# The first tile's result leaves by channels and comes back in squares of 32 tokens

## The chip, the core and the metric

The kernel runs on one core of a Trainium2 chip, as one program launched once. Five engines work side by side, each through a list of instructions of its own in a fixed order: TensorE (PE in the profile, its weight loads PEld), VectorE (DVE), ScalarE (ACT), GpSimd (POOL) and SyncE (SP). They wait for each other on semaphores. DMAs are issued from an engine's list, nearly all of them here from SyncE's. On-chip memory (SBUF, and PSUM for what TensorE writes) has 128 partitions. The metric is the device time of one execution in microseconds.

## What is computed

The reference is one step of a small streaming encoder of two layers, for a prompt of 1024 frames and a sample of 32 frames that share their weights. Rows are frames (tokens), columns are 1024 channels. Cut to what matters here:

```
def trunk(x, c, pool_cache, ...):
    for i in range(DEPTH):                       # 2 layers
        sh1, sc1, gt1, sh2, sc2, gt2 = split(silu(c) @ w_ada[i] + b_ada[i])
        h = rmsnorm(x, g_norm[i, 0]) * (1 + sc1) + sh1
        mix = sgu_mixer(h, ...) if i % 2 == 0 else pool_mixer(h, ...)
        x = x + gt1 * rmsnorm(mix, g_norm[i, 1])
        h = rmsnorm(x, g_norm[i, 2]) * (1 + sc2) + sh2
        f = square(relu(h @ ffn_w_up[i])) @ ffn_w_down[i]      # 1024 -> 4096 -> 1024
        x = x + gt2 * rmsnorm(f, g_norm[i, 3])
    return x
```

The last line of the loop, in the second layer, gives the outputs y_prompt (1024 x 1024) and y_sample (32 x 1024), rows of tokens. All values are 32-bit floats.

## The kernel before, in words

**Layout.** On chip the activations stand by channels: partition p of block k holds channel 128k + p, and the tokens lie along the free dimension. The tokens are cut into three tiles (TILES, L27): tile 0 and tile 1 of 384 prompt tokens, tile 2 of 256 prompt tokens and the 32 sample tokens. `acc[t]` holds the running sums of tile t, 8 blocks of 128 channels. The outputs are rows of tokens, so a result has to be turned once before it is written.

**The FFN, which is most of the time.** Each of its products runs as three matmuls of rounded parts (high times high, high times low, low times high), so that float precision is kept. The inner width of 4096 is cut into eight chunks of 512. One item (`ffn_item`, L1333) is one chunk for one tile: four `up` steps (pf, matmuls L917 to L919, then ScalarE's relu and square and a split into fh and fl), and a `down` of eight output blocks (pg), which VectorE adds into `acc`. The `down` of an item is issued after the first `up` of the next, so TensorE does not wait for the split. In layer 1 the last chunks, 6 and 7, go first for tiles 0 and 1, then for tile 2 (L344, L345). So the items at the end are: chunk 7 of tile 0, chunk 7 of tile 1, chunk 6 of tile 2, chunk 7 of tile 2.

**Weights.** They arrive in 512 KB pieces through three slots named raw (`t_raw`, L165, RAW_SLOTS) on SyncE's queue (L427); ScalarE makes the high part (L440), VectorE the low part. The same three raw slots also hold finished rows (yo) before they are written.

**The end of a tile.** After a tile's last `down`, `to_out` (L1614) puts a generator into `fillers`; its steps are recorded between the FFN's steps by `weave` and `pull`, which count TensorE's and VectorE's work in `time` and hold a step that yields a number back by so many counted microseconds. For tiles 0 and 1 the generator runs `residual` (L819): the norm's factor, the scaling of `acc`, and the addition of the old activations, which SyncE loads from DRAM in four pieces (xo_r, L826). Then, per block of 128 tokens, TensorE turns 8 squares of 128 x 128 into PSUM (yT, L1677), ScalarE copies them to a raw slot (yo, L1678), and SyncE writes 512 KB (L1679). That is 24 transpositions, six copies and three writes per tile.

**Tile 2** is last and goes another way (`last`, L1623). Its old activations were written by channels to DRAM scratch (xtd, L1437), are loaded back in squares of 32 tokens by 32 channels (`load_last`, L1395, nine loads) into the room that tile 0's inputs left, and VectorE turns each 32 x 32 square in place of TensorE (`turn_x`, L1405, VectorE's 32-wide transposition). The tile's sums are turned by TensorE while the last `down` runs (`turn_last`, L1420, yT at L1426). Once the norm's factor is known (r_last), one operation per half block scales and adds (xlast), and the rows are written (L1655, L1661).

**Buffers and order.** A buffer is named by a tag with a number of slots; a new buffer waits until the slot's last user is done. PSUM for transpositions has three slots (`ps_ms`, L142). Outside the hand-ordered opening, the framework's planner puts the recorded instructions in an order on each engine when the kernel is built, by costs and finishing times of its own; on the chip that order does not change. A DMA takes one of eight completion semaphores in turn, so it also waits for the DMA eight before it.

Of the kernel before, what the change touches and what calls it, by code (L numbers as in the profile page):

```python
# [9 lines left out]
F32 = mybir.dt.float32  # L10
# [5 lines left out]
P = 128  # L16
D = 1024
KB = D // P
# [5 lines left out]
HALO = 16  # L24
# [10 lines left out]
def tile_stream_encoder_step(  # L35
# [25 lines left out]
    nc = tc.nc  # L61
# [11 lines left out]
    def on_dve(op, fixed, rate):  # L73
        def run(out, *args, **kw):
            n = 1
            for k in out.shape[1:]:
                n *= k
            time["dve"] += fixed + n / rate
            return op(out, *args, **kw)  # L79

        return run
# [4 lines left out]
    turn32 = on_dve(nc.vector.transpose, 0.1, 930.0)  # L86
# [7 lines left out]
    dram = pool("dram", space=bass.MemoryType.DRAM)  # L94


    ncol = [p + s for _, p, s in TILES]
# [5 lines left out]
    acc = [const.tile([P, KB, HALO + n], F32, name=f"acc{t}") for t, n in enumerate(ncol)]  # L103
    xd = [dram.tile([P, KB, n], F32, name=f"xd{t}") for t, n in enumerate(ncol)]
    vd = dram.tile([SEQ + DEC, SGU], F32, name="vd")


    LAST = [(0, 0, P), (P, 0, P), (ncol[-1] - P, P - DEC, DEC)]
    xtd = dram.tile([32, 4, KB, ncol[-1]], F32, name="xtd")

    ident = const.tile([P, P], F32, name="ident")
    make_identity(nc, ident)
# [8 lines left out]
    part = const.tile([P, 4, NV, 8], F32, name="part")  # L121
# [11 lines left out]
    def room(part, t, name, dtype=F32):  # L133
        return work.tile([P, KB, ncol[t]], dtype, tag=f"h{part}{t}", bufs=1, name=name)
# [30 lines left out]
    def t_raw(name):  # L165
        return work.tile([P, 1024], F32, tag="raw", bufs=RAW_SLOTS, name=name)
# [652 lines left out]
    def residual(st, l, cf, tag, out, store=True, stat=True):  # L819
        t = st.t  # L820
        n = ncol[t]
        xos = {}

        def load(k2):
            xos[k2] = t_x(f"xo_{tag}_{k2}", [P, 2, n])
            nc.sync.dma_start(xos[k2], xd[t][:, 2 * k2 : 2 * k2 + 2, :])  # L826

        got = []
        yield from st.finish(got)
        r = got[0]  # L830
        st2 = Stat(t, tag + "x")
        for half in range(2):
            for k2 in (2 * half, 2 * half + 1):
                load(k2)
            for k2 in (2 * half, 2 * half + 1):
                for k in (2 * k2, 2 * k2 + 1):
                    for c0, w, v in segs[t]:
                        a = A(t, k, c0, w)
                        stt(
                            out=a,  # L840
                            in0=a,
                            scalar=coef[:, l, cf, v, k : k + 1],
                            in1=r[:, c0 : c0 + w],
                            op0=ALU.mult,
                            op1=ALU.mult,
                        )
                    yield True
                a = acc[t][:, 2 * k2 : 2 * k2 + 2, HALO:]
                tt(out=a, in0=a, in1=xos[k2], op=ALU.add)
                if stat:  # L850
                    st2.square(2 * k2, a)
                yield k2 % 2 == 0
        if store:
            nc.sync.dma_start(xd[t], acc[t][:, :, HALO:])
        out.append(st2)
# [246 lines left out]
    for half in range(2):  # L1102
        x = work.tile([P, 384], F32R, tag="rr", bufs=2, name=f"hs{half}")[:, : 8 * DEC].rearrange(
            "p (k n) -> p k n", k=4
        )
# [227 lines left out]
    def ffn_item(p, t, after):  # L1333
# [17 lines left out]
        def down():  # L1351
            for d in range(KB):
# [11 lines left out]
                if after is not None:  # L1364
                    st.square(d)
                    if l == 1 and t == NT - 1:
                        scale_last(d)
                        if d < len(LAST):
                            turn_x(d)
# [18 lines left out]

    last_ps = {}

    def rows_last(part, name):
        x = room(part, 0, name).rearrange("p k n -> p (k n)")
        return x.rearrange("p (b d) -> p b d", d=D)

    def load_last():  # L1395

        last_ps["raw"] = rows_last("l", "xraw")
        for i, (c0, r0, nr) in enumerate(LAST):
            for r in range(r0, r0 + nr, 32):
                nc.sync.dma_start(  # L1400
                    last_ps["raw"][r : r + 32, i].rearrange("p (j m) -> p j m", m=32),
                    xtd[:, :, :, c0 + r : c0 + r + 32].rearrange("s a k m -> s (a k) m"),
                )

    def turn_x(i):  # L1405
        if i == 0:
            last_ps["x"] = rows_last("h", "xlast")
        _, r0, nr = LAST[i]
        turn32(
            last_ps["x"][r0 : r0 + nr, i].rearrange("p (k a s) -> p a k s", k=KB, a=4),  # L1410
            last_ps["raw"][r0 : r0 + nr, i].rearrange("p (a k m) -> p a k m", a=4, k=KB),
        )

    def scale_last(d):
        t = NT - 1
# [4 lines left out]
    def turn_last(d):  # L1420
        half = d // 4
        for i, (c0, _, _) in enumerate(LAST):
            if d % 4 == 0:
# [6 lines left out]
    def mix_to_ffn(st, l):  # L1430
        t = st.t
        out = []
        need_ada(l, 2)
        yield from residual(st, l, 1, f"r1_{l}_{t}", out, store=l == 0 or t < NT - 1)
        if l == 1 and t == NT - 1:
            for a in range(4):
                nc.sync.dma_start(xtd[:, a], acc[t][32 * a : 32 * a + 32, :, HALO:])  # L1437
        need_ada(l, 4)
        yield from modulate(out[0], l, 2, 3)

# [173 lines left out]
    def to_out(st):  # L1614
        t = st.t
        col0, npr, nsm = TILES[t]
        blocks = [
            (c * P, P, y_prompt[0, col0 + c * P : col0 + (c + 1) * P, :]) for c in range(npr // P)
        ]
        if nsm:  # L1620
            blocks.append((npr, nsm, y_sample[0]))

        def last():  # L1623

            turn_last(KB - 2)
            pn = ps_dn("pn_last")
            nb = len(LAST)
            for k in (0, KB - 1):
                if k > 0:
                    turn_last(KB - 1)  # L1630
                for i, (c0, _, _) in enumerate(LAST):
                    mm(
                        pn[:, 2 * i : 2 * i + 2],
                        st.sq[:, k, c0 : c0 + P],
                        ones[:, 0:2],
                        start=k == 0 and i == 0,
                        stop=k > 0 and i == nb - 1,
                        skip_group_check=True,
                    )
            sums = pn[:, : 2 * nb].rearrange("p (b c) -> p b c", c=2)[:, :, 0]  # L1640
            r, q = (t_st(f"{x}_last")[:, :nb] for x in ("r", "q"))
            act(out=r, in_=sums, func=AF.Abs_reciprocal_sqrt, scale=1.0 / D)
            tt(out=q, in0=r, in1=r, op=ALU.mult)
            stt(out=q, in0=sums, scalar=-0.5 / D, in1=q, op0=ALU.mult, op1=ALU.mult)
            stt(out=r, in0=q, scalar=1.5, in1=r, op0=ALU.add, op1=ALU.mult)
            xt = last_ps["x"]
            dsts = [dst for _, _, dst in blocks]
            for i, (_, r0, nr) in enumerate(LAST):
                rows = slice(r0, r0 + nr)
                for half in range(2):  # L1650
                    d = slice(half * 512, half * 512 + 512)
                    y, x = last_ps[(i, half)][rows, :], xt[rows, i, d]
                    if nr == P:
                        stt(out=x, in0=y, scalar=r[rows, i : i + 1], in1=x, op0=ALU.mult, op1=ALU.add)
                        nc.sync.dma_start(dsts[i][:, d], x)  # L1655
                        continue

                    z = t_x(f"zlast{half}", [P, 512])[rows, :]
                    act(out=z, in_=y, func=AF.Copy, scale=r[rows, i : i + 1])
                    nc.gpsimd.tensor_tensor(out=x, in0=z, in1=x, op=ALU.add)  # L1660
                    nc.scalar.dma_start(dsts[i][:, d], x)  # L1661
            yield False

        def run():
            need_ada(1, 5)
            if t == NT - 1:
                yield from last()
                return
            yield from residual(st, 1, 3, f"r2_1_{t}", [], store=False, stat=False)
            yield 0.5  # L1670
            for c0, w, dst in blocks:
                tick(1.0)
                yo = t_raw(f"yo{t}_{c0}")
                for half in range(2):
                    pt = ps_ms(f"yT{t}_{c0}_{half}")
                    for i in range(4):
                        nc.tensor.transpose(pt[:w, i * P : (i + 1) * P], A(t, half * 4 + i, c0, w), ident)  # L1677
                    act(out=yo[:w, half * 512 : (half + 1) * 512], in_=pt[:w, :], func=AF.Copy)  # L1678
                nc.sync.dma_start(dst, yo[:w, :])  # L1679
                yield False  # L1680

        fillers.append((f"out_{t}", run()))

    run_ffn(1, to_out)
# [46 lines left out]
```

## Time and profile before

| | us |
|---|---|
| median of three runs | 2165.44 (2163.97 to 2165.93) |
| the profiled execution | 2163.59 |
| its span, first to last instruction | 2161.8 |
| TensorE busy in the span | 2143.9 (99%) |
| VectorE busy | 1423.9 (66%) |
| ScalarE busy | 981.9 (45%) |
| GpSimd busy | 7.9 |
| DMA | 311.77 MB, 144 GB/s on average |

In the profile's rows an operation is named by its source line, its engine, and out<-in by the program's buffer names; xN is a count. L79 is the line of a helper through which VectorE's operations pass, so names tell them apart. A row of the timeline begins with its start in the span and its length, and ends with the idle time ahead of it and what ended that. "SPq" is the issue of a DMA on SyncE's queue; landing is the time from issue until the DMA has signalled completion. Matmul lengths are modelled and overlap; the distance between the starts of two rows is the better measure of what a matmul costs.

### The profile page before, as it was taken

How to read it: one execution, taken by the hardware profiler on the slowest of the kernel's cores; microseconds unless marked ns; L12 is line 12 of the kernel's file. 1: busy time of each engine (PE TensorE's matmuls, PEld its weight loads, DVE VectorE, ACT ScalarE, POOL GpSimd, SP SyncE). 2: the span in 40 equal slices, each digit the busy share in tenths (PEclk: the TensorE clock that was granted, in tenths of full speed). 3: DMA queues.
4: the chain of work that ended last, by engine and by line, in shares of the span. 5: the costliest groups of instructions: out<-in, count | busy, mean ns of one | idle time of the engine just before them, and what ended most of it. 6: DMA issues, size and time to landing. Idle time of an engine off the chain costs nothing.

```text
span 2161.8 us, 33186 instructions
## 1 busy us (share of the span) xinstructions
PE 2143.9 (99%) x13214; PEld 2079.8 (96%) x13214; DVE 1423.9 (66%) x2520; ACT 981.9 (45%) x1667; POOL 7.9 (0%) x20
## 2 busy tenths in 40 slices
PE   8999999999999999999999999999999999999998
PEld 6878999999999999999999999999999999999998
DVE  6787738467778549576757779869685553523375
ACT  5634332233456652324345566656564542322454
POOL 0000000000000000000000000000000000000000
PEclk9999999999999999999999999999999999999999
DMA  8486524353447444344545466465454541302243
GB/s 299 153 269 209 168 82 136 96 153 107 133 126 220 127 147 146 98 117 137 175 127 164 143 192 200 148 193 164 141 161 133 166 149 58 108 20 69 78 137 120
DMA packets 363263, 311.77 MB, mean 144 GB/s; under 512 B 20099, under 2 KB 325803, under 8 KB 363109
## 3 DMA queue, kind: packets, MB, share of 16 engines
q1 hardware_dynamic: 362852, 309.43, 46.6%
q8 instruction: 103, 1.69, 0.3%
q14 instruction: 52, 0.42, 0.1%
q10 hardware_dynamic: 128, 0.14, 0.0%
q0 software_dynamic: 128, 0.09, 0.0%
HBM read 278.95 MB, written 30.66 MB: 143 GB/s over the span
## 4 chain that ended last, share of the span: by engine, by line
PE 96%; DVE 2%; DMA 1%; ACT 1%; issue 0%; POOL 0%; POOLq 0%; ACTq 0%; DVEq 0%
PE pf L917 11%; PE pg L917 11%; PE pf L919 11%; PE pf L918 11%; PE pg L919 11%; PE pg L918 11%; PE pu L917 3%; PE pu L919 3%; PE pu L918 3%; PE po L917 3%; PE po L918 3%; PE po L919 3%; PE pv L943 2%; PE pv L944 2%; PE pv L945 2%; PE psp L1263 1%
## 5 line engine op out<-in xcount | busy, mean ns | idle before, releaser
L917 PE MATMUL pg<-fh,wh_dn 128*128 128x384 f32 (+1 forms) x1536 | 496.1, 323 | 0.0
L917 PE MATMUL pf<-hh,wh_up 128*128 128x384 f32 (+1 forms) x1536 | 494.4, 322 | 0.0
L919 PE MATMUL pf<-hh,wl_up 128*128 128x384 f32 (+1 forms) x1536 | 493.0, 321 | 1.2 <-DVE wl_up L79 1.2
L918 PE MATMUL pf<-hl,wh_up 128*128 128x384 f32 (+1 forms) x1536 | 493.1, 321 | 0.0
L918 PE MATMUL pg<-fl,wh_dn 128*128 128x384 f32 (+1 forms) x1536 | 492.5, 321 | 0.0
L919 PE MATMUL pg<-fh,wl_dn 128*128 128x384 f32 (+1 forms) x1536 | 492.5, 321 | 0.0
L79 DVE TENSOR_TENSOR wl_up<-raw,wh_up 128x1024 fp32r<-128x1024 f32 x152 | 185.8, 1223 | 169.1 <-ACT wh_up L440 169.1
L919 PEld LDWEIGHTS pf<-hh,wl_up 128*128 128x128 f32 x1536 | 288.6, 188 | 1.9 <-DVE wl_up L79 1.9
L917 PEld LDWEIGHTS pg<-fh,wh_dn 128*128 128x128 f32 x1536 | 288.3, 188 | 1.5 <-ACT fh L1169 0.4
L440 ACT ACTIVATE wh_up<-raw 128x1024 fp32r<-128x1024 f32 x152 | 161.2, 1060 | 282.3 <-PE pf L918 217.7
L918 PEld LDWEIGHTS pg<-fl,wh_dn 128*128 128x128 f32 x1536 | 288.3, 188 | 0.9 <-DVE fl L79 0.2
L918 PEld LDWEIGHTS pf<-hl,wh_up 128*128 128x128 f32 x1536 | 288.3, 188 | 0.4
L917 PEld LDWEIGHTS pf<-hh,wh_up 128*128 128x128 f32 x1536 | 288.2, 188 | 0.4
L919 PEld LDWEIGHTS pg<-fh,wl_dn 128*128 128x128 f32 x1536 | 288.2, 188 | 0.0
L79 DVE TENSOR_TENSOR acc<-acc,pg 128x384 f32<-128x384 f32 (+1 forms) x336 | 173.7, 517 | 151.2 <-PE pg L919 150.5
L440 ACT ACTIVATE wh_dn<-raw 128x1024 fp32r<-128x1024 f32 x152 | 160.9, 1060 | 209.8 <-PE pg L918 171.4
L79 DVE TENSOR_TENSOR wl_dn<-raw,wh_dn 128x1024 fp32r<-128x1024 f32 x152 | 185.8, 1223 | 82.7 <-ACT wh_dn L440 82.6
L79 DVE SCALAR_TENSOR_TENSOR aa<-raw,csil,aa 128x512 f32<-128x512 f32 (+1 forms) x364 | 203.2, 619 | 7.6 <-DMA raw<-in_w_ada_dram 7.3
L1345 ACT ACTIVATE r<-pf 128x384 f32<-128x384 f32 (+1 forms) x192 | 86.5, 450 | 197.7 <-PE pf L919 197.7
L79 DVE TENSOR_TENSOR fl<-r,fh 128x384 fp32r<-128x384 f32 (+1 forms) x192 | 100.0, 521 | 85.7 <-ACT fh L1169 84.2
L917 PE MATMUL pu<-hh,wh_u 128*128 128x384 f32 (+1 forms) x384 | 125.9, 328 | 0.0
L917 PE MATMUL po<-ush,wh_o 128*128 128x384 f32 (+1 forms) x384 | 123.5, 322 | 0.0
(268 smaller groups left out, 2923.2 us busy)
## 6 DMA issues: line engine op xcount, KB each, us to landing
raw<-in_ffn_w_up_dram SPq DMA_DIRECT2D x152, 512.0 KB, 3.9
raw<-in_ffn_w_down_dram SPq DMA_DIRECT2D x152, 512.0 KB, 3.5
raw<-in_w_ada_dram SPq DMA_DIRECT2D x96, 512.0 KB, 4.4
raw<-in_sgu_w_in_dram SPq DMA_DIRECT2D x40, 512.0 KB, 4.2
xd<-acc SPq DMA_DIRECT2D x8, 1536.0 KB, 7.8
raw<-in_sgu_w_out_dram SPq DMA_DIRECT2D x24, 512.0 KB, 3.6
xo_r<-xd SPq DMA_DIRECT2D x32, 384.0 KB, 3.3
vd<-vt SPq DMA_DIRECT2D x32, 256.0 KB, 4.3
```

Of the source, the lines that this page charges most:

```text
L79: return op(out, *args, **kw)
L440: act(out=wh, in_=r, func=AF.Copy)
L917: mm(ps[:, :n], wh, rh, start=i == 0, stop=False)
L918: mm(ps[:, :n], wh, rl, start=False, stop=False)
L919: mm(ps[:, :n], wl, rh, start=False, stop=i == last)
L943: mm(ps[:m, :], a_h, wh[:, o : o + 512], start=k == 0, stop=False)
L944: mm(ps[:m, :], a_h, wl[:, o : o + 512], start=False, stop=False)
L945: mm(ps[:m, :], a_l, wh[:, o : o + 512], start=False, stop=k == KB - 1)
L1263: mm(sp[:, c * P : (c + 1) * P], vl[:, c, k * P : (k + 1) * P], wr[:, c * P : (c + 1) * P], start=True, stop=True,)
L1345: act(out=r[:, :n], in_=ps[:, :n], func=AF.Relu)
```

## The change

Only `run` in `to_out` behaves otherwise, and only for tile 0. After its `residual` the result is written by channels to a new DRAM buffer `yd` in four DMAs of 384 KB (`by_channels`). The generator yields 8.0, then loads the result back in squares of 32 tokens, four loads of 128 KB for each of three blocks (`squares`), into `yraw`, the room that tile 1's inputs hh use until then. It yields 8.0 again, then VectorE turns each block into a raw slot (`turn_rows`) and SyncE writes it, 512 KB. The 24 transpositions and six copies of tile 0 are gone. The helpers are taken out of the code for tile 2, which issues what it did before.

```
+    yd = dram.tile([32, 4, KB, ncol[0]], F32, name="yd")
...
+    def by_channels(dst, t):
+        for a in range(4):
+            nc.sync.dma_start(dst[:, a], acc[t][32 * a : 32 * a + 32, :, HALO:])
+
+    def squares(dst, src, c0):
+
+        nc.sync.dma_start(
+            dst.rearrange("p (j m) -> p j m", m=32),
+            src[:, :, :, c0 : c0 + 32].rearrange("s a k m -> s (a k) m"),
+        )
+
+    def turn_rows(dst, src):
+        turn32(
+            dst.rearrange("p (k a s) -> p a k s", k=KB, a=4),
+            src.rearrange("p (a k m) -> p a k m", a=4, k=KB),
+        )
+
+    def rows_of(part, t, name):
+        x = room(part, t, name).rearrange("p k n -> p (k n)")
         return x.rearrange("p (b d) -> p b d", d=D)
...
             yield from residual(st, 1, 3, f"r2_1_{t}", [], store=False, stat=False)
+            if t == 0:
+                by_channels(yd, t)
+                yield 8.0
+                raw = rows_of("h", 1, "yraw")
+                for i, (c0, _, _) in enumerate(blocks):
+                    for r in range(0, P, 32):
+                        squares(raw[r : r + 32, i], yd, c0 + r)
+                yield 8.0
+                for i, (c0, _, dst) in enumerate(blocks):
+                    yo = t_raw(f"yo{t}_{c0}")
+                    turn_rows(yo, raw[:, i])
+                    nc.sync.dma_start(dst, yo)
+                    yield False
+                return
             yield 0.5
             for c0, w, dst in blocks:
                 tick(1.0)
```

More of the change, by code (lines that the diff above doesn't have):

```diff
@@ L1389, in tile_stream_encoder_step @@
     last_ps = {}
-    def rows_last(part, name):
-        x = room(part, 0, name).rearrange("p k n -> p (k n)")
+    def by_channels(dst, t):
[13 more added lines that the diff above has]
+        x = room(part, t, name).rearrange("p k n -> p (k n)")
         return x.rearrange("p (b d) -> p b d", d=D)
     def load_last():
-        last_ps["raw"] = rows_last("l", "xraw")
+        last_ps["raw"] = rows_of("l", 0, "xraw")
         for i, (c0, r0, nr) in enumerate(LAST):
             for r in range(r0, r0 + nr, 32):
[L1400 to L1403, printed above, removed]
+                squares(last_ps["raw"][r : r + 32, i], xtd, c0 + r)
     def turn_x(i):
         if i == 0:
-            last_ps["x"] = rows_last("h", "xlast")
+            last_ps["x"] = rows_of("h", 0, "xlast")
         _, r0, nr = LAST[i]
[L1409 to L1412, printed above, removed]
+        turn_rows(last_ps["x"][r0 : r0 + nr, i], last_ps["raw"][r0 : r0 + nr, i])
     def scale_last(d):
@@ L1435, in mix_to_ffn @@
         if l == 1 and t == NT - 1:
-            for a in range(4):
-                nc.sync.dma_start(xtd[:, a], acc[t][32 * a : 32 * a + 32, :, HALO:])
+            by_channels(xtd, t)
         need_ada(l, 4)
```

## The prediction

> **What bounds the kernel now.** I read the page first (engines, then the chain that ended last), then that chain in order of time over the last 120 us, then TensorE's timeline there. From the page:
>
> ```profile
> span 2161.8 us, 33186 instructions
> PE 2143.9 (99%) x13214; PEld 2079.8 (96%) x13214; DVE 1423.9 (66%) x2520; ACT 981.9 (45%) x1667; POOL 7.9 (0%) x20
> PE 96%; DVE 2%; DMA 1%; ACT 1%; issue 0%; POOL 0%; POOLq 0%; ACTq 0%; DVEq 0%
> ```
>
> TensorE's stream is the chain for 96% of the span, so a TensorE instruction removed ahead of the last product is worth its slot, and anything put behind the last product is paid in full. The chain's end, start and length in us:
>
> ```profile
> 2142.13 0.66 PE yT L1426 x6
> ...
> 2149.77 0.66 PE yT L1426 x6
> 2152.04 0.47 DVE acc L79
> 2152.53 0.45 ACT sq_rf L761
> 2153.03 0.84 PE pn_last L1632 x6
> ...
> 2155.63 1.27 POOL xlast L1660
> 2156.90 1.23 POOLq L1727
> ```
>
> The last product (pg) is followed by VectorE's addition, the norm (pn_last), the final scaling (xlast), and the writes. In the timeline:
>
> ```profile
> 2151.71 0.29 PE L919 MATMUL pg<-fh,wl_dn 128*128 128x288 f32 x1
> ...
> 2154.77 2.73 DVE L79 SCALAR_TENSOR_TENSOR xlast<-yT,r_last,xlast 128x512 f32<-128x512 f32 x4
> ```
>
> I call the start of the first scaling A. Before, A is 2154.77 and the span ends at 2161.8, A+7.0.
>
> **What TensorE loses.** Its timeline around the row transpositions (yT), x is the count:
>
> ```profile
> 2108.51 1.47 PE L1677 MATMUL yT<-ident,acc 128*128 128x128 f32 x12
> 2109.74 0.38 PE L917 MATMUL pg<-fh,wh_dn 128*128 128x288 f32 x1
> ...
> 2111.14 0.29 PE L918 MATMUL pg<-fl,wh_dn 128*128 128x288 f32 x1
> 2111.64 1.14 PE L1677 MATMUL yT<-ident,acc 128*128 128x128 f32 x8 [0.21 <-ACT yo L1678]
> 2112.54 0.38 PE L919 MATMUL pg<-fh,wl_dn 128*128 128x288 f32 x1
> ...
> 2116.84 0.60 PE L1677 MATMUL yT<-ident,acc 128*128 128x128 f32 x4
> 2117.20 0.42 PE L806 MATMUL pn_rf<-sc_rf,ones 128*128 128x384 f32 x1
> ...
> 2134.19 1.47 PE L1677 MATMUL yT<-ident,acc 128*128 128x128 f32 x12
> ...
> 2135.82 0.66 PE L1677 MATMUL yT<-ident,acc 128*128 128x128 f32 x4 [0.15 <-ACT yo L1678]
> 2136.23 0.38 PE L917 MATMUL pg<-fh,wh_dn 128*128 128x288 f32 x1
> ...
> 2136.71 1.07 PE L1677 MATMUL yT<-ident,acc 128*128 128x128 f32 x8
> 2137.53 0.38 PE L917 MATMUL pg<-fh,wh_dn 128*128 128x288 f32 x1
> ```
>
> Tile 0's 24 (the first three groups) hold TensorE 2108.51 to 2109.74 = 1.23, from the end of the product's slot (2111.14 + 0.13) to 2112.54 = 1.27 (a wait for ScalarE is in it), and 0.36. The first product after a group is longer by 0.09, twice. Sum 3.0 us, with 12 in 1.23 = 0.103 a transposition.
>
> That is not all that moves. The program's order on each engine is fixed by a planner when the kernel is built, and the built order of the changed kernel differs in its last 400 instructions. Three things are pushed behind the last product: 20 of tile 1's 24 transpositions; the addition of the old activations for the second half of tile 1's channels (two VectorE additions); and three of tile 2's six half blocks. VectorE's end, and SyncE's queue ahead of it, now stand like this:
>
> ```
> VectorE: xlast<-yT x2 | acc<-acc,xo_r | acc<-acc,xo_r | yo<-yraw (turn) | yo<-yraw (turn)
>          | xlast<-yT | yo<-yraw (turn) | xlast<-yT
> SyncE:   last weight load | xraw<-xtd x4 | yraw<-yd x12 | xo_r<-xd x2
>          | out<-xlast x2 | out<-yo x4 | out<-xlast | out<-yo x2 | out<-xlast
> ```
>
> So before the last product TensorE also loses tile 1's pieces. Its 24 take 2134.19 to 2136.23 and 2136.71 to 2137.53, with switches 3.0; of these, four transpositions with a switch (0.5) stay, and I allow 0.25 for a wait for fh that the 20 had covered: 2.25 saved. Of tile 2's transpositions 18 stood ahead of the last product (three sixes, first and last quoted above), now 10 in smaller groups: 8 x 0.103 less two switches = 0.65. A comes 3.0 + 2.25 + 0.65 = 5.9 us earlier, at 2148.9. ScalarE loses six evictions of 0.6 and is not the bound there: nothing.
>
> **What the new path costs ahead of A.** Rows for the squares (xraw is the same form as the twelve new loads; issue time, then landing), and the two rows that set when SyncE gets there:
>
> ```profile
> L1400 SPq DMA_DIRECT2D xraw<-xtd x9: 550/551/1015, 2066.3 to 2112.5; - x9
> ...
> DMA to landing us min/median/max: 2.8/3.8/4.9
> ```
>
> ```profile
> 2109.67 1.23 DVE L79 TENSOR_TENSOR wl_dn<-raw,wh_dn 128x1024 fp32r<-128x1024 f32 x1 [1.49 <-ACT wh_dn L440]
> ```
>
> The last weight load waits for that split's raw slot, so about 2110.9; 16 squares at 0.55 to 1.02 follow, until 2120 to 2127; the two loads xo_r behind them land by 2132 at the latest. VectorE reads them at A+1.4 = 2150: 18 us or more of cover, nothing paid. If it were gone, every later write would wait as well, because they stand behind on the same queue. The four writes by channels stand among the last weight loads; no row shows them here, and the nearest, squares and loads, give 0.55 to 1.02 of queue each, 2 to 4 us, while the last weights have from 2111 to the products after 2137. Nothing paid; the range keeps 1 us for it.
>
> **The tail.** Groups of instructions, mean ns after the comma:
>
> ```profile
> L79 DVE TENSOR_TENSOR acc<-acc,xo_r 128x768 f32<-128x768 f32 x8 | 7.6, 950 | 0.0
> L1678 ACT ACTIVATE yo<-yT 128x512 f32<-128x512 f32 x12 | 6.4, 598 | 0.9 <-DVE wl_dn L79 0.8
> L79 DVE STREAM_TRANSPOSE xlast<-xraw 128x1024 f32<-128x1024 f32 (+1 forms) x3 | 3.7, 1238 | 0.0
> L79 DVE SCALAR_TENSOR_TENSOR xlast<-yT,r_last,xlast 128x512 f32<-128x512 f32 x4 | 2.7, 744 | 0.0
> L1677 PE MATMUL yT<-ident,acc 128*128 128x128 f32 x48 | 6.4, 276 | 0.4 <-ACT yo L1678 0.4
> ```
>
> The writes of 512 KB, their landing, and the rate in slices of 0.25 us from 2136 while three are under way:
>
> ```profile
> L1679 SPq DMA_DIRECT2D out_dram<-yo x6: 332/338/357, 2112.1 to 2138.6; - x6
> ...
> DMA to landing us min/median/max: 2.6/2.9/5.1
> ```
>
> ```profile
> GB/s 0 0 0 0 0 115 410 459 426 393 410 410 459 410 393 393 393 459 459 377 262 0 16 16 16 16 33 33 0 0 0 0 0 0 0 0 0 0 0 0
> ...
> out_dram<-yo SPq DMA_DIRECT2D x3, 512.0 KB, 3.5
> ```
>
> Three take 4.0 us of slices: 1.33 each, 0.67 for 256 KB; the first bytes come 0.8 after the first issue. And the last bytes of the run, slices of 0.1 us from 2157.8:
>
> ```profile
> GB/s 430 369 348 348 246 307 348 205 226 369 431 389 389 410 410 348 185 164 246 123 82 21 0 0 0 0 0 0 0 0 0 0 0 0 0 0 0 0 0 0
> ```
>
> They stop at 2160.0, 1.8 before the end. From A, the new path goes: two scalings 1.4; two additions, 3.3; two transpositions of tile 1 and one latency (0.27), 3.7; ScalarE's eviction 0.6, 4.3; the write of tile 1's first block 2.9 until it lands, 7.2, because only its landing frees the raw slot that VectorE's second turn writes; that turn 1.24, 8.4; a scaling 0.74, 9.15; the third turn, 10.4; the last scaling, 11.1. (The first turn is hidden in the wait; tile 1's last block, behind GpSimd's two additions and ScalarE's two write issues, is ready at about 10.7.) From 8.4 on five writes leave within 2.7 us, 512, 256, 512, 512 and 256 KB: bytes from 9.2, for 5.3 us, until 14.5; with 1.8 after them the end is A+16.3. Nine changes of engine at 0.04 (2152.04 + 0.47 to 2152.53 and 2152.53 + 0.45 to 2153.03 in the chain give 0.02 and 0.05) add 0.36.
>
> Clock: granted clock is the fraction behind the POOL column.
>
> ```profile
> 2150.00:2152.00 2.00, 2.00 (x18) 2.00 (x17) 0.72 (x2) 1.17 (x3) 0.00 (x0) 1.00 0.00 0
> 2154.50:2161.80 7.30, 0.00 (x0) 0.00 (x0) 2.92 (x6) 1.25 (x2) 2.50 (x2) 0.69 0.45 163
> ```
>
> With TensorE idle it falls from 1.00 to a mean of 0.69. The two transpositions on the tail's path and their latency (0.47) would cost between 0 and 0.47 more; I take half, 0.25. The Trainium skill (TensorE: Matmul & The Clock Gate, Part 1) says the clock is half after an idle window of about 3.4 us and full only after a busy one; by it the sum would hold the whole 0.47, +0.2 on mine, and the 0.69 agrees with a fall to half some way into the stretch.
>
> Sum: tail 16.3 + 0.36 + 0.25 - 7.0 = +9.9; with -5.9, **+4.0 us**. The profiled execution took 2163.59 with a span of 2161.8, 1.85 below the median shown; on the median 2165.44 this is 2169.4. About 0.2% (4.3 us) is what a measurement of this kernel can tell from no change, so the forecast lies just inside: a little slower.
>
> **Rivals.** *Clearly slower*: tile 1's first write lands as late as the slowest row of its kind, 5.1 instead of 2.9, since two more 512 KB writes are issued within 1.3 us behind it. Everything from the second turn on moves by 2.2: +6.2, 2171.6. It decides from a landing of 3.2 on; the three issued together have a median of 3.5, which speaks for it, and the minimum of 2.6 against it. *Milder*: the five last writes do not share a rate. Tile 1's last block, issued at 10.7, then has its last bytes 0.8 + 1.33 later, at A+12.8, and the end is A+14.6; with 0.36 and 0.25 for changes of engine and clock that is +2.3, 2167.7. The slices near 400 GB/s speak against it. *Faster*: only the removal counts and the tail stays as long as before: -3.0, 2162.4. It would need tile 1's second half ahead of the last product; the built order excludes that, unless TensorE's earlier part gains more than its slots, and the group of yT above shows no more than 0.4 us of idle time ahead of its matmuls.
>
> **How the numbers follow.** Forecast 0.55, with its own range 2167.9 to 2171.0 (landing 2.6 to 3.5, clock, 1 us of queue); slower rival 0.27; milder 0.14; faster 0.04. Of the forecast's range I put four tenths above +4.3: slower 0.22 + 0.27 = 0.49, the same 0.33 + 0.14 = 0.47, faster 0.04. The range takes both neighbours and the spread of the runs (1 us): 2166.5 to 2173.5.
>
> **What the profile after would show.** Right: no yT for tile 0; last product near 2145.8; VectorE's two acc<-acc,xo_r behind the second xlast; the second turn (yo<-yraw) released by a write landing; the span's end near A+17. Wrong if the last product is not 5 us or more earlier (a weight came late behind the channel writes), if xo_r lands after A+1.4, or if the tail after A is under 14 us.

## The result and the profile after

The changed kernel takes 2169.27 us (median of 11 runs, 2168.52 to 2170.13) against 2163.44 us before (11 runs, 2162.86 to 2165.93): ratio 1.0026, 95% interval 1.0018 to 1.0033, so 5.8 us slower (3.9 to 7.1 by the interval). Measured once more on another occasion it was 1.0027 (1.0017 to 1.0036). The forecast was 2169.4, by +4.0 on a median of 2165.44 from three runs. The profiled execution has a span of 2167.4, 5.6 more than before. From its page:

```profile
span 2167.4 us, 33154 instructions
PE 2145.0 (99%) x13190; PEld 2079.7 (96%) x13190; DVE 1426.8 (66%) x2523; ACT 978.7 (45%) x1661; POOL 8.0 (0%) x20
```

The busy times say nothing of the loss: TensorE executes 24 instructions fewer and its modelled busy time is 1.1 longer, but the same sum over the identical program ahead of the mark below differs by 3.7 between the profiles of this study (2060.4 to 2064.1). To see where the time went, one needs a mark that does not move. Up to the norm of tile 0 (its matmul pn_rf on sc_rf) all kernels here run the same program, but executions differ in the time at which they reach it: from 2069.70 to 2073.79 in the profiles of this study. So each profile is read from that mark. Before, from its timeline:

```profile
2071.38 0.34 PE L806 MATMUL pn_rf<-sc_rf,ones 128*128 128x384 f32 x1
```

A, the first final scaling, was at 2154.77: 83.39 from the mark, and 7.03 from A to the end. The timeline of the changed kernel, mark first, then the rows that answer to the prediction's tail:

```profile
2071.60 0.34 PE L808 MATMUL pn_rf<-sc_rf,ones 128*128 128x384 f32 x1
...
2146.37 0.29 PE L921 MATMUL pg<-fh,wl_dn 128*128 128x288 f32 x1
...
2148.44 0.33 PE L1438 MATMUL yT<-ident,acc 128*128 128x128 f32 x1
...
2149.42 1.41 DVE L79 SCALAR_TENSOR_TENSOR xlast<-yT,r_last,xlast 128x512 f32<-128x512 f32 x2
...
2150.75 1.82 DVE L79 TENSOR_TENSOR acc<-acc,xo_r 128x768 f32<-128x768 f32 x2
2151.75 4.53 PE L1702 MATMUL yT<-ident,acc 128*128 128x128 f32 x20 [2.98 <-DVE acc L79]
...
2153.54 1.67 ACT L1703 ACTIVATE yo<-yT 128x512 f32<-128x512 f32 x3 [4.82 <-PE yT L1702]
2154.16 1.40 SPq L1704 DMA_DIRECT2D out_dram<-yo  x2
...
2156.91 1.25 DVE L79 STREAM_TRANSPOSE yo<-yraw 128x1024 f32<-128x1024 f32 x1 [3.19 <-DMA out_dram<-yo]
...
2161.05 1.08 ACT L1703 ACTIVATE yo<-yT 128x512 f32<-128x512 f32 x2 [2.58 <-DVE yo L79]
2162.16 0.33 SPq L1704 DMA_DIRECT2D out_dram<-yo  x1
2162.59 0.41 SPq L1666 DMA_DIRECT2D out_dram<-xlast  x1
```

A is at 2149.42, 77.82 from the mark: 5.57 earlier than before. The end is A+17.98: 10.95 later than before. 10.95 - 5.57 = 5.4, which is the loss behind the mark (the spans differ by 5.6; the mark itself came 0.2 later). The two additions (acc<-acc,xo_r), 20 of tile 1's transpositions, and behind them the copies and six writes of 512 KB stand after the last product (pg), as the built order had it. Two things are to be seen: the 20 transpositions take 4.53, 0.23 each, against 12 in 1.23 before; and the second turn waits 3.19 for a write of tile 1 to land.

The chain that ended last, in order of time, goes another way than the wait for that write:

```profile
2151.75 4.53 PE yT L1702 x20
2156.28 0.87 PE yT L1438 x4
2157.22 0.69 ACT zlast L1670
2158.05 1.26 POOL xlast L1671
2159.31 1.25 POOLq L1752
2160.58 0.37 ACTq L1672
2161.05 0.60 ACT yo L1703
2161.65 0.49 ACTq L1752
```

Tile 2's last twelve transpositions (yT L1438) queue behind tile 1's twenty on TensorE; ScalarE's zlast waits for the first four of them, GpSimd's additions wait for zlast, ScalarE's write issues wait for GpSimd, and the copies of tile 1's last block stand behind those on ScalarE. It is ready at 2162.13, A+12.7. The granted clock (first number of the last three) in some stretches, with TensorE's modelled busy time behind the length of each:

```profile
2150.50:2151.00 0.50, 0.00 (x0) 0.00 (x0) 0.50 (x2) 0.00 (x0) 0.00 (x0) 0.62 0.00 0
2157.00:2158.00 1.00, 0.18 (x2) 0.05 (x1) 1.00 (x1) 0.78 (x2) 0.00 (x0) 0.77 1.04 426
...
2147.20:2150.60 3.40, 1.24 (x9) 0.96 (x8) 1.66 (x5) 1.32 (x4) 0.00 (x0) 1.00 0.00 0
2150.60:2154.00 3.40, 2.25 (x11) 2.25 (x12) 3.12 (x4) 0.46 (x1) 0.00 (x0) 0.50 0.40 154
2154.00:2157.40 3.40, 3.13 (x15) 2.71 (x13) 0.49 (x1) 1.39 (x4) 0.00 (x0) 0.50 0.73 300
...
2160.00:2161.00 1.00, 0.12 (x2) 0.00 (x0) 1.00 (x2) 0.00 (x0) 0.55 (x1) 0.93 0.93 297
```

It halves at about 2150.6 (mean 0.62 in the slice from 2150.5), 1.8 after TensorE's last instruction ended (2148.44 + 0.33), is full again only from about 2157.5 (mean 0.77), when nearly all transpositions are done, and halves once more at about 2160.9 (mean 0.93). The Trainium skill (TensorE: Matmul & The Clock Gate, Part 1) has the clock fall after an idle window of about 3.4 us, and says that these windows run freely, without regard to the program. The trace agrees: the three changes (2150.62, 2157.46 and 2160.86 by these means) lie 6.8 and 3.4 apart, the 3.4 us before the first fall hold 1.24 of modelled TensorE work, the 3.4 before the rise 3.13, and the 3.4 between them, with 2.25, change nothing. So the 1.8 is no threshold: in the second profile of this kernel (after_again) the fall comes 1.5 after TensorE's last instruction (0.71 in the slice 2148.5 to 2149.0, the instruction's end at 2147.25), in the kernel before 3.1 (0.66 in the slice 2157 to 2158, 2154.24). And in slices of 0.5 us from 2148, the bytes of the last writes:

```profile
GB/s 0 0 0 0 0 0 356 389 303 0 0 0 0 0 451 418 418 410 410 442 418 180 442 410 291 303 299 274 332 393 377 369 401 381 168 33 0 0 0 0
```

From 2155 to 2165.5 the queues are hardly ever empty. So by this profile two chains run side by side to the end, the serial one through TensorE, ScalarE and GpSimd, and the writes. The experiments take them apart.

### The profile page after: what moved, and what is told of

Read it like the earlier page. It is cut to its first block, busy times and chain, and to the rows that moved or that the text cites. A ratio compares the mean times of both kernels' runs of the same rounds, so it can differ in the third digit from the quotient of the medians.

```text
span 2167.4 us, 33154 instructions
## 1 busy us (share of the span) xinstructions
PE 2145.0 (99%) x13190; PEld 2079.7 (96%) x13190; DVE 1426.8 (66%) x2523; ACT 978.7 (45%) x1661; POOL 8.0 (0%) x20
## 4 chain that ended last, share of the span: by engine, by line
PE 96%; DVE 2%; DMA 1%; ACT 1%; issue 0%; POOLq 0%; POOL 0%; ACTq 0%; DVEq 0%
PE pf L919 11%; PE pf L921 11%; PE pf L920 11%; PE pg L919 11%; PE pg L921 11%; PE pg L920 11%; PE pu L919 3%; PE pu L921 3%; PE pu L920 3%; PE po L920 3%; PE po L919 3%; PE po L921 3%; PE pv L945 2%; PE pv L946 2%; PE pv L947 2%; PE psp L1265 1%
```

## The experiments

Times are medians of 11 runs (8 for own_room, 5 for xo_on_act), each beside runs of the kernel before on the same chip (there 2163.14 to 2163.50). "Mark to A" and "A to end" are from one profile each, as above. The medians tell a microsecond apart only roughly; the two distances, which repeat to 0.01 in after and after_again, tell more.

| kernel | us | ratio to before (95%) | mark to A | A to end |
|---|---|---|---|---|
| before | 2163.44 | | 83.39 | 7.03 |
| after | 2169.27 | 1.0026 (1.0018, 1.0033) | 77.82 | 17.98 |
| after_again | 2168.66 | 1.0027 (1.0017, 1.0036) | 77.81 | 17.99 |
| no_out0 | 2161.60 | 0.9990 (0.9982, 0.9999) | 80.29 | 6.91 |
| xo_on_act | 2173.34 | 1.0042 (1.0029, 1.0055) | 80.03 | 18.98 |
| own_rows_act | 2165.38 | 1.0010 (1.0001, 1.0019) | 84.03 | 7.54 |
| split_queues | 2160.05 | 0.9986 (0.9977, 0.9995) | 80.10 | 6.82 |
| split_again | 2159.40 | 0.9984 (0.9975, 0.9993) | 80.09 | 6.85 |
| before_xo_act | 2163.92 | 1.0003 (0.9995, 1.0012) | 83.38 | 7.14 |
| warm24 | 2168.34 | 1.0021 (1.0013, 1.0030) | 77.82 | 17.15 |
| own_room | 2169.46 | 1.0028 (1.0017, 1.0038) | 77.81 | 18.29 |
| no_writes0 | 2167.14 | 1.0018 (1.0010, 1.0027) | 77.80 | 16.41 |
| warm_no_writes0 | 2165.42 | 1.0008 (0.9999, 1.0017) | 77.82 | 14.61 |

My theory was that the removal is worth its 3 us, and that the order in the last stage, not the detour through DRAM, turns it into a loss. The rivals: the detour's own traffic costs the time; or one thing in the tail does (slot wait, write rate, clock).

### What the removal is worth: no_out0

```
             yield 0.5
+            if t == 0:
+                return
             for c0, w, dst in blocks:
```

> The kernel before with tile 0's result left out altogether: neither transposed, evicted nor written (its part of the output stays unwritten). It gives the price of what the change removes, without what it adds. My theory, that the 24 slots are worth 3.0 us on TensorE and that the order of the last stage is the same as before: 2163.4 - 3.0 = 2160.4, the last scaling 3.0 earlier than at 2154.77, tail still 7.0. Rival, that the slots were filled with something else anyway: 2162.5 to 2163.5.

```profile
2072.00 0.34 PE L806 MATMUL pn_rf<-sc_rf,ones 128*128 128x384 f32 x1
...
2152.29 2.73 DVE L79 SCALAR_TENSOR_TENSOR xlast<-yT,r_last,xlast 128x512 f32<-128x512 f32 x4
```

Mark to A fell by 3.10, against the 3.0 worked out for the 24 slots; the tail stayed. The median fell by 1.9 (interval 0.2 to 3.9), between theory and rival; the distances in the profile agree with the theory.

### The two late loads alone: xo_on_act

```
-            nc.sync.dma_start(xos[k2], xd[t][:, 2 * k2 : 2 * k2 + 2, :])
+            queue = nc.scalar if tag == "r2_1_1" and k2 > 1 else nc.sync
+            queue.dma_start(xos[k2], xd[t][:, 2 * k2 : 2 * k2 + 2, :])
```

> The changed kernel with one thing undone: the two loads of old activations for the second half of tile 1 (xo_r) are issued on ScalarE's queue, so that they do not stand behind the squares on SyncE's. Built order: tile 1's two additions and its 24 transpositions stand ahead of the last product again, one turn and two more stand among and behind the four scalings. My theory, that the position of these two loads makes the long tail: A near 2151.2, VectorE's last turn ends A+6.8, eight writes share the rate until about A+9.5, end A+11: 2163.5, between 2161.5 and 2166. Rival, that the detour's own traffic or the three late turns and writes cost the time: 2168 or more.

The theory's time did not come: 2173.34 is 9.8 slower than before, the slowest of all, and lies where the rival put it. Half of the theory held all the same: mark to A is 80.03, as without tile 0's transpositions, and VectorE has both additions done 24 us before the last product (2147.96):

```profile
2120.32 0.95 DVE L79 TENSOR_TENSOR acc<-acc,xo_r 128x768 f32<-128x768 f32 x1
2122.85 0.96 DVE L79 TENSOR_TENSOR acc<-acc,xo_r 128x768 f32<-128x768 f32 x1
...
2159.08 1.25 DVE L79 STREAM_TRANSPOSE yo<-yraw 128x1024 f32<-128x1024 f32 x1 [3.56 <-DMA out_dram<-yo]
```

But SyncE's queue stood still. Its issues, and what it waited for (total, times, longest):

```profile
2120.33 35.00 SPq L1400 DMA_DIRECT2D yraw<-yd  x12
```

```profile
SPq L1400 <- DMA out_dram<-xlast: 24.5, 1, 24.5
```

The twelfth square waited 24.5 us for a write of xlast that ScalarE issues after A (at 2153.13). In the trace both signal the same one of the eight completion semaphores, so this is the wait for the DMA that had the semaphore before: the planner had placed the last square behind that write, though on the chip nothing else held the queue. So tile 1's finished rows, and tile 0's turns behind the slots they held, went out after 2155: late turns and writes, as the rival says, but late by this wait and not by traffic. In the changed kernel the same twelve squares were issued in 11.33 (2118.41 to 2129.74), because there the eight DMAs before each one are early ones.

### All squares on ScalarE's queue: own_rows_act

```
-        nc.sync.dma_start(
+        (queue or nc.sync).dma_start(
...
-                        squares(raw[r : r + 32, i], yd, c0 + r)
+                        squares(raw[r : r + 32, i], yd, c0 + r, nc.scalar)
...
+                rows = rows_of("l", 1, "yrows")
...
-                    yo = t_raw(f"yo{t}_{c0}")
+                    yo = rows[:, i]
```

> The changed kernel with the twelve squares issued on ScalarE's queue and the turned rows in a room of their own instead of raw slots. Built order: everything of tile 0 and tile 1 stands ahead of the last product, the tail is four scalings as before. My theory: A 3.0 to 3.6 earlier than 2154.77 and a tail of 7: 2160.2, plus what ScalarE's twelve issues of 0.55 to 1.02 (eleven of them in a row, 6 to 11 us) take from TensorE where it waits for the hidden layer's activations, 0 to 5: 2160 to 2165. Rival, that the detour's traffic costs the time whatever the order: 2168 or more.

The tail is short again (7.54) with the whole detour done, so the rival (2168 or more) falls, though the time is 0.4 above the theory's range. Mark to A is 84.03 instead of 80.1, and ScalarE's and TensorE's timelines show why:

```profile
2125.67 8.21 ACTq L1399 DMA_DIRECT2D yraw<-yd  x10
2133.99 0.71 ACT L1347 ACTIVATE r<-pf 128x288 f32<-128x288 f32 x2 [7.87 <-DMA yraw<-yd]
...
2135.74 0.53 PE L919 MATMUL pg<-fh,wh_dn 128*128 128x288 f32 x2 [1.75 <-ACT fh L1171]
...
2136.56 2.82 PE L1703 MATMUL yT<-ident,acc 128*128 128x128 f32 x12
2139.04 0.59 PE L921 MATMUL pg<-fh,wl_dn 128*128 128x288 f32 x1
```

```profile
2136.40:2139.70 3.30, 3.30 (x16) 3.16 (x17) 1.22 (x2) 2.56 (x6) 0.00 (x0) 0.50 0.86 343
```

ScalarE issued ten squares for 8.2 us with the relu of two up steps behind them; TensorE waited 1.75 for their result. Then the granted clock was at half from 2136.4 to 2139.8, though TensorE was at work again since 2135.74, and its next 12 transpositions took 2.48 (2136.56 to 2139.04), twice the 1.23 of before.

### Six and six, with the loads ahead: split_queues, split_again

```
-                        squares(raw[r : r + 32, i], yd, c0 + r)
+                        squares(raw[r : r + 32, i], yd, c0 + r, nc.scalar if 4 * i + r // 32 >= 6 else nc.sync)
```

The two loads xo_r are moved as in xo_on_act, and the turned rows have a room of their own as in own_rows_act.

> The changed kernel with its whole detour, but six of the twelve squares issued on SyncE's queue and six on ScalarE's, the two late loads xo_r of tile 1 on ScalarE's queue ahead of them, and the turned rows in a room of their own. Built order: tile 1's additions, all its transpositions and the three turns ahead of the last product, no DMA waits for a completion of a later stage, the tail is four scalings as before. My theory, that order and not the detour costs the time: A 2151.2 to 2152, ScalarE's four issues in a row taking 0 to 1 from TensorE, tail 7.0 to 7.5: 2160.5 to 2162.0. Rival, that the detour itself (its traffic, VectorE's turns, the issues) costs what the removal saves: 2163.0 or more.

> The kernel split_queues once more, beside the control: 2159.5 to 2161.0, 2 to 3.5 below the control if the detour with its order kept is what gains; equal to the control if the moved loads alone gain.

2160.05 and 2159.40, 3.1 and 3.8 us faster than before and a little below both ranges (by 0.45 and 0.1): the detour, kept whole, gains when the order is kept. From split_again:

```profile
2125.70 2.72 ACTq L1400 DMA_DIRECT2D yraw<-yd  x4
...
2132.56 1.24 DVE L79 STREAM_TRANSPOSE yrows<-yraw 128x1024 f32<-128x1024 f32 x1
...
2143.09 1.24 DVE L79 STREAM_TRANSPOSE yrows<-yraw 128x1024 f32<-128x1024 f32 x1
...
2150.55 2.72 DVE L79 SCALAR_TENSOR_TENSOR xlast<-yT,r_last,xlast 128x512 f32<-128x512 f32 x4
```

The turns lie beside the products, ScalarE's four issues hold it for 2.7 and no longer reach TensorE, and the tail is the four scalings as before. Mark to A, 80.1, is no longer than that of no_out0 (80.29), where there is no detour at all: its traffic, turns and issues cost nothing ahead of A.

### The control: before_xo_act and after_again

The edit of xo_on_act in the kernel before; and the changed kernel itself, on the chip of split_again.

> The kernel before with one change: tile 1's two late loads xo_r on ScalarE's queue, as in the kernel split_queues, without the detour. The control: how much of split_queues' gain the moved loads bring by themselves. My theory, nothing, since these loads do not stand on the chain before: 2162.5 to 2164.0. Rival, that they are the gain: 2160 to 2161.

> The changed kernel once more, so that it stands beside the other three on one chip: 2168.5 to 2170, tail 17 to 18.5 from A.

The moved loads by themselves bring nothing (1.0003). The changed kernel repeats itself to 0.01 us in both distances.

### The clock: warm24

```
+            warm = ps_dn("warm")
+            for i in range(24):
+                nc.tensor.transpose(warm[:, (i % 4) * P : (i % 4 + 1) * P], ident, ident)
```

> The changed kernel with 24 transpositions of the identity added behind the last product, ten of them ahead of the last transposition of tile 2, the others just behind it; their result is not used. They keep TensorE busy until about 2.3 us before tile 1's transpositions. If the half clock makes the tail longer than forecast: tile 1's 20 take 2.1 to 2.5 us instead of 4.53, the last four 0.45 instead of 0.87, and the end comes 2.0 to 2.9 earlier less 0.4 to 1.0 for the ten ahead: 2167.0 to 2168.5. Rival, that the writes' landing and rate set the end: 2169.3 to 2170.3, with the transpositions short all the same.

```profile
2150.88 3.14 PE L1705 MATMUL yT<-ident,acc 128*128 128x128 f32 x20 [0.89 <-DVE acc L79]
...
2154.59 1.25 ACT L1673 ACTIVATE zlast<-yT,r_last 32x512 f32<-32x512 f32 x2 [0.80 <-issue]
...
2150.00:2155.00 5.00, 3.38 (x24) 2.53 (x24) 2.85 (x3) 1.98 (x4) 0.00 (x0) 1.00 0.55 218
```

The time lies in the range of the theory. The clock stays at 1.00, the 20 transpositions take 3.14 instead of 4.53 (2.1 to 2.5 were expected), zlast starts at A+6.0 (A is 2148.55) instead of A+7.8. The end comes 0.83 earlier, less than the 1.8 that the chain gained. The medians, each against the kernel before on its chip, fell by 1.0, which their intervals do not separate. Even at full clock the 20 take 0.157 each, more than the 0.103 of before; so the clock is 1.4 of their 4.53, and no run shows what the rest is.

### The writes: own_room, no_writes0, warm_no_writes0

own_room is the `rows` edit above alone. no_writes0 drops `nc.sync.dma_start(dst, yo)` behind `turn_rows`. warm_no_writes0 is no_writes0 and warm24 together.

> The changed kernel with the turned rows of tile 0 in a room of their own (the one that tile 1's inputs hl left) instead of the three raw slots, so that no turn waits for a write of tile 1 to land. The loads keep their order; tile 1's two additions and 20 transpositions stay behind the last product, with the three turns among them, and the four writes of xlast now come last on SyncE's queue. If the wait of 3.19 us for the slot is what makes the tail long: end near A+15, 2166.0 to 2167.5. If the bytes of the last writes set it: all are issued between A+5 and A+14, 3 MB at about 400 GB/s, no gain, 2168.3 to 2170.

> The changed kernel without the three final writes of tile 0 (its rows are turned, but never written, so this part of the output is missing); the order of tile 1 and tile 2 stays that of the changed kernel. No slot waits for a landing of tile 1's, and 1.5 MB fewer leave at the end. If write rate and landing make the tail long: two scalings, two additions, three turns, two scalings on VectorE, end near A+13, 2164 to 2165.5. If the serial work of tile 1's second half makes it (additions, 20 transpositions at half clock, evictions): end near A+15 to A+16, 2166.5 to 2168.

> The changed kernel without tile 0's three final writes and with the 24 idle transpositions behind the last product: both edits together (this part of the output is missing). What is left is the serial work of tile 1's second half at full clock. If the half clock is paid in full where writes do not cover it: the 20 transpositions shrink by 1.4 to 2.4, the last twelve by 0.8 to 1.2, so 2.0 to 3.0 below the kernel without the writes alone: 2164.0 to 2165.2. Rival, that the clock costs no more than the 1 us seen with the writes in place: 2166.0 to 2167.0.

own_room gained nothing, but it does not tell what the slot's wait costs: the planner put the three turns ahead of tile 1's additions, which therefore came 3.4 later:

```profile
2148.83 3.49 DVE L79 STREAM_TRANSPOSE yrows<-yraw 128x1024 f32<-128x1024 f32 x3
...
2152.24 1.78 DVE L79 TENSOR_TENSOR acc<-acc,xo_r 128x768 f32<-128x768 f32 x2
```

In no_writes0 the order of tile 1 and tile 2 is that of the changed kernel; slot wait and 1.5 MB are gone:

```profile
2154.65 3.79 DVE L79 STREAM_TRANSPOSE yo<-yraw 128x1024 f32<-128x1024 f32 x3
...
2159.39 1.25 ACT L1670 ACTIVATE zlast<-yT,r_last 32x512 f32<-32x512 f32 x2 [2.01 <-PE yT L1438]
...
2162.01 1.08 ACT L1702 ACTIVATE yo<-yT 128x512 f32<-128x512 f32 x2 [1.36 <-POOL xlast L1671]
```

The turns run through, and still zlast starts at A+7.8 and tile 1's last copies at A+10.4 (A is 2151.59). The end is A+16.4: wait and bytes together are worth 1.57, and the serial work is most of the tail. In warm_no_writes0, with the clock kept up as well, the span ends at 2162.9:

```profile
2148.29 1.41 DVE L79 SCALAR_TENSOR_TENSOR xlast<-yT,r_last,xlast 128x512 f32<-128x512 f32 x2
```

That is A+14.61. So the clock costs 0.83 where the writes stand beside it and 1.80 where they do not (2.0 to 3.0 were expected), and both together 3.37, which is more than 0.83 + 1.57: each hides a part of the other. What is left, 14.61 - 7.03 = 7.6 us, comes with tile 1's second half behind the last product: its additions, transpositions, copies and writes. No run takes these apart; where the order keeps them ahead of it (split_queues), the tail is 6.82.

## Why the prediction was right, and where not

**The absolute time: luck.** 2169.4 against 2169.27 looks exact, but the forecast stood on a median of three runs, 2165.44, and eleven runs of the same kernel gave 2163.44. This 2.0 too much made up for a change that was forecast 1.8 too small (+4.0 against +5.8).

**TensorE's removal: right.** 3.0 for tile 0's 24 was 3.10 (no_out0). For all that leaves TensorE ahead of A, 5.9 was predicted and 5.57 measured; the 0.3 belongs to the part for tiles 1 and 2 (2.9, measured 2.47). No run separates its cause.

**Nothing paid ahead of A: right.** split_again's mark to A is no longer than that of no_out0. The estimates inside were not as good. SyncE's rows in the changed kernel:

```profile
2111.82 6.48 SPq L1399 DMA_DIRECT2D xraw<-xtd  x4
2118.41 11.33 SPq L1399 DMA_DIRECT2D yraw<-yd  x12
2129.78 1.16 SPq L828 DMA_DIRECT2D xo_r<-xd  x2
```

A square took 0.94 of the queue and xraw 1.62, so the two loads were issued until 2130.9, later than the 2120 to 2127 worked out for the squares. They landed 4.4 after their issue, still 15 before the additions.

**The tail: right in kind, 1.05 too short, and by a chain that is not the one that ends last.** In steps, predicted and measured from A: additions done 3.3 and 3.15; tile 1's first write issued 4.3 and 4.74; second turn starts 7.2 and 7.49, so this write landed 2.75 after its issue, against 2.9; third turn done 10.4 and 11.13; tile 1's last block ready 10.7 and 12.71; end 16.9 and 17.98. The step that failed is the clock on the path that ends last: I charged half speed for two transpositions and a latency, 0.25, because only these stood on the path that I followed, through the landing and the turns. All 20, and tile 2's behind them, run at half speed, and zlast, GpSimd and the last copies wait for them: by warm24 1.8 late at that point and 0.83 at the end. The 0.47 that I worked out by the rule of the Trainium skill (TensorE: Matmul & The Clock Gate, Part 1) fell short for the same reason. The landing's 2.9 was a real wait, but by no_writes0 it and 1.5 MB of writes together decide only 1.57 of the end. That the sum still came within 1.05 is in part luck: the chain that I followed and the one that I left out are nearly as long, for without the wait and those bytes the end is still A+16.41.

**The rivals.** The clearly slower one needed a landing of 3.2 or more for tile 1's first write; it was 2.75. Against the milder one (writes share no rate) speak the slices of the last writes: 274 to 442 GB/s from 2159 to 2165, with several under way. The faster one, 2162.4, was excluded because it "would need tile 1's second half ahead of the last product". That was the right condition: where split_queues meets it, the time is 2160.05.

**What made the order.** That the two loads behind the squares on SyncE's queue are the cause is shown by xo_on_act, where moving them alone brings the additions back to 2120. Why the planner places the squares so late is not settled; xo_on_act shows only that its order has the last one behind ScalarE's write of xlast, a wait of 24.5 us in which nothing else held SyncE's queue.

## What to carry to other kernels

Work taken off the bounding engine gained its slots here only where what replaced it left the order of the last stage alone; compare the built orders first, and measure each profile from a mark ahead of the change. A DMA can be late with nothing else in its queue, when its completion semaphore was last given to a DMA of a later stage (24.5 us in xo_on_act), so moving one load to another queue can stop a third. A wait of TensorE can cost twice, once as a wait and once as half speed of what follows (the tail of the changed kernel, and own_rows_act after a wait of 1.75).

## What was not expected

- The granted clock halved 1.8 us after TensorE's last instruction and stayed at half for 6.8 us, though TensorE was busy again from 2151.75; in own_rows_act it halved only after TensorE had resumed. 24 transpositions with an unused result kept it at 1.00.
- One wait for a completion semaphore held a queue for 24.5 us in which nothing else did.
- Read from the mark, two profiles of one kernel agree to 0.01 us in each distance (after, after_again, 95.8 us in all), while their spans differ by 1.5; the difference arises ahead of the mark (2071.60 and 2070.10). The granted clock fell at another point of the tail in the two (0.4 us apart from A), but the 20 transpositions lay within the stretch at half in both.
